# SwiGLU's first product by one level of Strassen's algorithm, its rows in five chunks, in a hybrid decoder trunk on one core

## The chip, the cores and the metric

One core of one Trainium2 chip runs the whole program. The metric is the device time of one execution in microseconds (us); the time before is the median of three runs. The engines are named as the profile names them: PE (TensorE matmul), PEld (TensorE weight load), DVE (VectorE), ACT (ScalarE), POOL (GpSimd), SP (SyncE, which issues the loads).

## The reference

A trunk of two layers over 512 tokens of width 1024, in float32. Layer one is a gated linear recurrence (RG-LRU) and a SwiGLU; then keys and values are computed once; layer two is a dilated attention and a second SwiGLU. The change is in both SwiGLUs:

```python
D_MODEL, SEQ = 1024, 512
FFN_HIDDEN = -(-8 * D_MODEL // (3 * 256)) * 256          # 2816

def swiglu(h, w_in, w_out):
    g, u = jnp.split(h @ w_in, 2, axis=-1)
    return (jax.nn.silu(g) * u) @ w_out

    ...
        h = h + swiglu(rms_norm(h, a_ffn_norm[i]), a_ffn_w_in[i], a_ffn_w_out[i])
```

## The kernel before

Everything is kept transposed: rows (features) on the 128 partitions, the 512 tokens along the free axis. The residual `h` is eight tiles 128x512, one for each 128 features. A float32 product is made of three products of a short float32 format: a value is split into a high half (a cast, ACT) and a low half (value minus high half, mostly DVE), and `mm3` issues high x high, high x low and low x high into one PSUM tile. `split` and `halve` make these halves for activations (`split` also multiplies by the norm's gain), `Stream._split` for weights.

The weights come as one long list of pieces (`add_pieces`), 128x1024 each or less. `Stream` loads them in that order through SP into two buffers `wr` (`_load`), two pieces ahead; one piece ahead it casts the high half `wh` on ACT (L92) and subtracts for the low half `wl` on DVE (L94), or on POOL for pieces marked `pool_lo`. There are three buffers each of `wh` and `wl`.

`swiglu` (L422) runs over 22 blocks `j` of 128 hidden rows. For each it computes the gate block and the up block, 8 x 3 = 24 matmuls 128x512 each (the first product), multiplies each by `rb` (the norm's factor for every token) on DVE, takes silu on ACT (L441), the product on POOL (L443), and splits the result into `gh[j]`, `gl[j]` (L203, L204). After all blocks `out_proj` (L238) runs over 8 blocks `m` of output features, each with 22 x 3 matmuls 128x512 (the second product), adds the PSUM tile to `h[m]` on DVE (L249) and calls `after(m)`, which splits and squares `h[m]` for the next stage or stores it. So an FFN has 1056 matmuls in the first product and 528 in the second, all of 512 columns, and the program has two FFNs.

The stage ahead of FFN1 is the `a_out` projection; its `after_a` splits `h[m]` into `xh`, `xl`. The stage ahead of FFN2 is `out_half(1)`, the second half of the attention's output projection (L823, added on DVE at L833), and then eight `split` calls. A tile framework orders each engine's instructions from the program text and priorities (weight splits run at high priority) and sets the semaphores; pools of buffers decide when a buffer is free again.

Of the kernel before, what the change touches and what calls it, by code (L numbers as in the profile page):

```python
# [23 lines left out]
T = 512  # L25
KB = 8
HID = 2816
HB = HID // 128
EPS = 1e-6
# [33 lines left out]

class Stream:
# [8 lines left out]
    def _load(self, i):  # L73
        ap = self.pieces[i][0]
# [3 lines left out]
        return [lambda c=c: self.nc.sync.dma_start(r[:, c], ap[:, c]) for c in self._cuts(i, w)]  # L78
# [4 lines left out]
    def _split(self, i):  # L83
        nc = self.nc
        r, w = self.raw.pop(i)
        hi = self.pool.tile([128, 1024], F32R, name=f"wh{i}", tag="wh")
        lo = self.pool.tile([128, 1024], F32R, name=f"wl{i}", tag="wl")
        self.parts[i] = (hi, lo)

        def do(c):  # L90
            with self.tc.high_priority():
                nc.scalar.copy(hi[:, c], r[:, c])  # L92
                eng = nc.gpsimd if self.pieces[i][1] else nc.vector
                eng.tensor_tensor(lo[:, c], r[:, c], hi[:, c].bitcast(F32), ALU.subtract)  # L94

        return [lambda c=c: do(c) for c in self._cuts(i, w)]

# [25 lines left out]
def trunk(tc, A, out):  # L123
# [3 lines left out]
    def mm3(ps, w, x, first, last):  # L127
        (wh, wl), (xh, xl) = w, x
        PE.matmul(ps, wh, xh, start=first, stop=False)  # L129
        PE.matmul(ps, wh, xl, start=False, stop=False)  # L130
        PE.matmul(ps, wl, xh, start=False, stop=last)  # L131
# [3 lines left out]
    def add_pieces(aps, pool_lo=False):  # L135
        start = len(pieces)
        pieces.extend((a, pool_lo) for a in aps)
# [4 lines left out]
    add_pieces([A["w_in"][m] for m in lru_order[2:]], True)  # L142
# [7 lines left out]
    p_f1 = ffn_pieces("f1_in", "f1_out")  # L150
    p_kv = add_pieces([A["w_kv"][i] for i in range(12)])
    p_q = add_pieces([A["w_q"][i] for i in range(24)], True)
    p_o = add_pieces([A["w_o"][i] for i in range(8)], True)
    p_f2 = ffn_pieces("f2_in", "f2_out")

    with tc.tile_pool(name="keep", bufs=1) as kp, tc.tile_pool(name="wts", bufs=3) as wp, \
# [96 lines left out]
        with tc.tile_pool(name="lru", bufs=2) as lp:  # L253
# [126 lines left out]
            hgh = [lp.tile([128, T], F32R, name=f"hgh{k}", bufs=1) for k in range(KB)]  # L380
            hgl = [lp.tile([128, T], F32R, name=f"hgl{k}", bufs=1) for k in range(KB)]
# [33 lines left out]
            def after_a(m):  # L415
                split(h[m], gain(C_AF, m), xh[m], xl[m])
                squares(m, lp, "q", 2)

            out_proj(p_aout, KB, KB, hgh, hgl, after_a)


        def swiglu(fp, p, after):  # L422
            gh = [fp.tile([128, T], F32R, name=f"gh{j}", bufs=1) for j in range(HB)]
            gl = [fp.tile([128, T], F32R, name=f"gl{j}", bufs=1) for j in range(HB)]
            for j in range(HB):
                pair = []
                for i in range(2):
                    ps = bank()
                    wh, wl = ws.get(p[0] + 2 * j + i)
                    for k in range(KB):  # L430
                        c = slice(128 * k, 128 * k + 128)
                        mm3(ps, (wh[:, c], wl[:, c]), (xh[k], xl[k]), k == 0, k == KB - 1)
                    pair.append(ps)
                    if j == 0 and i == 0:
                        r = norm_factors(fp)
                if j == 0:
                    rb = norm_rows(fp, r)
                g = fp.tile([128, T], F32, name="g")
                u = fp.tile([128, T], F32, name="u")
                V.tensor_tensor(g, pair[0], rb, ALU.mult)  # L440
                S.activation(g, g, AF.Silu)  # L441
                V.tensor_tensor(u, pair[1], rb, ALU.mult)  # L442
                G.tensor_tensor(u, u, g, ALU.mult)  # L443
                halve(u, gh[j], gl[j])
            out_proj(p[1], HB, 8, gh, gl, after)

        with tc.tile_pool(name="ffn1", bufs=2) as fp:
            fp = Pool(fp)

            def after_f1(m):  # L450
                split(h[m], gain(C_KV, m), xh[m], xl[m])
                squares(m, fp)

            swiglu(fp, p_f1, after_f1)


        with tc.tile_pool(name="att", bufs=2) as ap:
            ap = Pool(ap)
            attention(tc, A, ap, ws, dict(locals()))

        with tc.tile_pool(name="ffn2", bufs=2) as fp:
            fp = Pool(fp)

            def after_f2(m):
                nc.sync.dma_start(out[m], h[m])

            swiglu(fp, p_f2, after_f2)
# [9 lines left out]
def attention(tc, A, ap, ws, env):  # L477
# [388 lines left out]


    for _ in out_half(1, lambda m: env["squares"](m, ap, "qh", 3)):
        pass
    for m in range(8):  # L870
        split(h[m], gain(C_BF, m), xh[m], xl[m])
# [70 lines left out]
```

## Time and profile before

| what | value |
|---|---|
| time before, median of 3 runs (lowest, highest) | 1300.27 us (1297.78 to 1300.62) |
| the profiled execution | 1298.5 us |
| its span in the trace | 1296.7 us |
| PE busy | 1234.9 us, 95% |
| DVE busy | 733.3 us, 57% |
| ACT busy | 512.5 us, 40% |
| POOL busy | 234.3 us, 18% |
| moved by DMA | 112.98 MB, mean 87 GB/s |

The recurrent stage takes the first 150 us or so and `a_out` some 50 us behind it, FFN1 lies from about 200 to 560 us, keys, values and attention up to about 910, and FFN2 from there to the end. A row of a group reads: line, engine, operation, output and inputs, shape, count, then busy time, the mean of one in ns, and idle time ahead of it with what ended it. A matmul's own duration is longer than the distance to the next, since they are pipelined; what counts is the distance between starts, called pitch below.

### The profile page before, as it was taken

The page shows a single profiled execution, that of the slowest core. Times are in us where ns is not written, and L with a number is a line of the kernel's source. Part 1 is how long each engine was busy: PE and PEld are TensorE (multiplying, and loading weights), DVE is VectorE, ACT ScalarE, POOL GpSimd, SP SyncE. Part 2 cuts the span into 40 slices and gives each one's busy share as a digit, 9 for nine tenths or more (in the row PEclk, how much of TensorE's full clock was granted, in tenths as well). Part 3 has the DMA queues.
Part 4 walks back from the last instruction along what each step waited for, and adds up shares of the span by engine and source line. Part 5 has one row for each costly group of instructions (what it writes and reads, how often), then busy time and mean ns, then how long its engine had stood idle before and what let it go on. Part 6 is the DMA issues. An engine that isn't in the chain of part 4 may idle for free.

```text
span 1296.7 us, 14893 instructions
## 1 busy us (share of the span) xinstructions
PE 1234.9 (95%) x5634; PEld 1015.9 (78%) x5634; DVE 733.3 (57%) x1294; ACT 512.5 (40%) x950; POOL 234.3 (18%) x186
## 2 busy tenths in 40 slices
PE   6778899999999999999998899899999999999998
PEld 5556688888888888887877677789888888888887
DVE  7889865555544434367655666876755445552221
ACT  5466643233332223256444455654433322232120
POOL 1443100111111000010333354531111111110000
PEclk8888899999999999999998999799999999999999
DMA  5221222333333333332322211101223333233341
GB/s 179 83 65 49 66 98 92 92 94 96 98 98 98 90 99 97 104 108 97 114 82 65 82 50 65 33 17 34 86 93 98 98 98 96 90 93 108 106 122 53
DMA packets 35494, 112.98 MB, mean 87 GB/s; under 512 B 4320, under 2 KB 6496, under 8 KB 35424
## 3 DMA queue, kind: packets, MB, share of 16 engines
q1 hardware_dynamic: 34416, 110.17, 27.4%
q10 hardware_dynamic: 1008, 1.88, 0.5%
q8 instruction: 44, 0.72, 0.2%
q14 instruction: 26, 0.21, 0.1%
HBM read 108.89 MB, written 2.10 MB: 86 GB/s over the span
## 4 chain that ended last, share of the span: by engine, by line
PE 79%; DVE 14%; ACT 5%; issue 2%; DMA 0%; SPq 0%; POOL 0%; ACTq 0%; DVEq 0%; POOLq 0%
PE ps L131 22%; PE ps L130 22%; PE ps L129 22%; PE ps L633 3%; PE ps L634 3%; PE ps L635 3%; DVE kn L592 3%; DVE xc L328 1%; ACT junk L575 1%; DVE gated L377 1%; PE ps L708 1%; PE ps L778 1%; ACT wh L92 1%; DVE pr L763 1%; DVE cl L204 1%
## 5 line engine op out<-in xcount | busy, mean ns | idle before, releaser
L92 ACT CAST wh<-wr 128x1024 fp32r<-128x1024 f32 (+2 forms) x206 | 210.9, 1025 | 524.1 <-PE ps L130 452.7
L129 PE MATMUL ps<-xh,wh 128*128 128x512 f32 x896 | 356.6, 398 | 6.7 <-ACT xh L199 6.0
L131 PE MATMUL ps<-xh,wl 128*128 128x512 f32 x896 | 355.1, 396 | 0.0
L130 PE MATMUL ps<-xl,wh 128*128 128x512 f32 x896 | 352.5, 393 | 0.0
L94 DVE TENSOR_TENSOR wl<-wr,wh 128x1024 fp32r<-128x1024 f32 (+2 forms) x160 | 234.1, 1464 | 155.0 <-ACT wh L92 154.8
L129 PEld LDWEIGHTS ps<-xh,wh 128*128 128x128 f32 x896 | 170.5, 190 | 43.5 <-ACT xh L199 6.0
L130 PEld LDWEIGHTS ps<-xl,wh 128*128 128x128 f32 x896 | 170.4, 190 | 38.8 <-issue 0.7
L131 PEld LDWEIGHTS ps<-xh,wl 128*128 128x128 f32 x896 | 170.3, 190 | 37.5
L94 POOL TENSOR_TENSOR wl<-wr,wh 128x1024 fp32r<-128x1024 f32 x46 | 113.8, 2474 | 253.1 <-ACT wh L92 181.1
L443 POOL TENSOR_TENSOR u<-u,g 128x512 f32<-128x512 f32 x44 | 58.4, 1326 | 508.6 <-ACT wh L92 368.2
L129 PE MATMUL ps<-gh,wh 128*128 128x512 f32 x352 | 137.0, 389 | 0.0
L131 PE MATMUL ps<-gh,wl 128*128 128x512 f32 x352 | 136.9, 389 | 0.0
L130 PE MATMUL ps<-gl,wh 128*128 128x512 f32 x352 | 136.9, 389 | 0.0
L442 DVE TENSOR_TENSOR u<-ps,rb 128x512 f32<-128x512 f32 x44 | 30.4, 691 | 141.1 <-PE ps L131 141.1
L633 PE MATMUL ps<-wh,xh 128*128 128x512 f32 x224 | 93.6, 418 | 0.0
L635 PE MATMUL ps<-wh,xl 128*128 128x512 f32 x224 | 89.7, 401 | 0.0
L634 PE MATMUL ps<-wl,xh 128*128 128x512 f32 x224 | 89.7, 400 | 0.0
L130 PEld LDWEIGHTS ps<-gl,wh 128*128 128x128 f32 x352 | 66.1, 188 | 13.8
L131 PEld LDWEIGHTS ps<-gh,wl 128*128 128x128 f32 x352 | 66.1, 188 | 13.7
L129 PEld LDWEIGHTS ps<-gh,wh 128*128 128x128 f32 x352 | 66.1, 188 | 13.7
L440 DVE TENSOR_TENSOR g<-ps,rb 128x512 f32<-128x512 f32 x44 | 30.4, 691 | 66.5 <-PE ps L131 66.5
L203 ACT CAST gh<-u 128x512 fp32r<-128x512 f32 x44 | 27.3, 621 | 60.2 <-POOL u L443 60.2
(211 smaller groups left out, 1591.9 us busy)
## 6 DMA issues: line engine op xcount, KB each, us to landing
wr<-in_f_in SPq DMA_DIRECT2D x88, 512.0 KB, 3.5
wr<-in_f_out SPq DMA_DIRECT2D x32, 512.0 KB, 3.5
wr<-in_w_q SPq DMA_DIRECT2D x24, 512.0 KB, 3.5
wr<-in_w_in SPq DMA_DIRECT2D x14, 512.0 KB, 3.5
wr<-in_f_out SPq DMA_DIRECT2D x16, 384.0 KB, 3.1
wr<-in_w_kv SPq DMA_DIRECT2D x12, 512.0 KB, 3.5
wr<-in_a_out SPq DMA_DIRECT2D x8, 512.0 KB, 3.5
wr<-in_w_o SPq DMA_DIRECT2D x8, 512.0 KB, 3.5
```

Source lines behind the costliest of these rows:

```text
L92: nc.scalar.copy(hi[:, c], r[:, c])
L94: eng.tensor_tensor(lo[:, c], r[:, c], hi[:, c].bitcast(F32), ALU.subtract)
L129: PE.matmul(ps, wh, xh, start=first, stop=False)
L130: PE.matmul(ps, wh, xl, start=False, stop=False)
L131: PE.matmul(ps, wl, xh, start=False, stop=last)
L440: V.tensor_tensor(g, pair[0], rb, ALU.mult)
L442: V.tensor_tensor(u, pair[1], rb, ALU.mult)
L443: G.tensor_tensor(u, u, g, ALU.mult)
L592: V.scalar_tensor_tensor(dst[:, c], dst[:, c], r[:, nh * t + i:nh * t + i + 1], grow[:, g_row, :], ALU.mult, ALU.mult)
L633: PE.matmul(ps[t], xh[k][:, r], wh[:, c], start=k == 0, stop=False)
L634: PE.matmul(ps[t], xh[k][:, r], wl[:, c], start=False, stop=False)
L635: PE.matmul(ps[t], xl[k][:, r], wh[:, c], start=False, stop=k == 7)
```

## The change

The first product of a hidden block `j` becomes a "unit": the gate block and the up block are the two rows of a 2x2 block matrix, whose columns are the even and the odd input features k (blocks of 128); the tokens 0 to 255 and 256 to 511 are the two columns of the right side. Winograd's form of Strassen's algorithm makes the four results out of seven products: A11·B11, S1·T1, S2·T2, A12·B21, S3·T3, A22·T4, S4·B22, where S1 to S4 are sums of weight blocks and T1 to T4 sums of activation blocks. Each product is 4 pairs of k x 3 matmuls of 256 columns, so a unit has 84 matmuls 128x256 in place of 48 of 128x512.

The products are summed in two PSUM banks and a third takes A12·B21; three sums are copied out by ACT while their bank goes on accumulating (`copied`, 128x256: t1, t2, t3), and DVE adds them to the other products. The products A22·T4 and S4·B22 of a unit (`tail`) come after the first two products of the next unit (`head`). `rb` now multiplies the gate (up to its silu) and, for the up half, the output of the second product (`out_end`), so each output step takes two DVE steps, a product into `o` and an addition to `h[m]`, 40 times in an FFN, where before there were 8 additions.

For the weights of a unit DVE makes the four S sums (128x512 each) and their low halves (two of 128x1024), ACT their high halves. The low halves of A11, A12 and A22 are made without DVE: ACT writes the negated raw value's rounding (L135), and a DMA issued by POOL adds the raw weights to it, read once more from DRAM (L136: 512 KB into `wl`, 256 KB into `a2l`). For the activations `sums` makes T1 to T4 and their halves from pairs of `h` tiles; it takes the place of `split` ahead of both FFNs.

The hidden blocks come in chunks of 4, 5, 5, 4 and 4. The second product of chunk c runs between the units of chunk c+1, one or two output blocks `m` after each unit (matmuls 128x512, 12 or 15 to an output block); the last chunk's eight stand at the end. The pools of the stages overlap (`reuse_waits="tile"`, a pool on the right side for `hgh`, `hgl`, `gh`, `gl`).

```diff
+CHUNKS = (4, 5, 5, 4, 4)
...
+    def _load_unit(self, i):
+        g = self.pool.tile([128, 1024], F32, name=f"wr{i}", tag="wr", bufs=2)
+        u = self.unit_pool.tile([128, 1024], F32, name=f"ur{i}", tag="ur", bufs=1)
...
+    def _split_unit(self, i):
...
+        def negated_plus(lo, raw, ap):
+            nc.scalar.mul(lo, raw, -1.0)
+            nc.gpsimd.dma_start(lo, ap, accum_op=ALU.add)
...
+            (a11, a12), (a21, a22) = ([halves(t)[:, e] for e in range(2)] for t in (g, u))
+            negated_plus(a1l, g, self.pieces[i][0][0])
+            negated_plus(a2l, a22, halves(self.pieces[i][0][1])[:, 1])
+            nc.scalar.copy(a1h, g)
+            nc.scalar.copy(a2h, a22)
...
+            for n in range(2):
+                if n == 0:
+                    V.tensor_tensor(s[0][:, 0], a21, a22, ALU.add)
+                    V.tensor_tensor(s[0][:, 1], s[0][:, 0], a11, ALU.subtract)
+                else:
+                    V.tensor_tensor(s[1][:, 0], a11, a21, ALU.subtract)
+                    V.tensor_tensor(s[1][:, 1], a12, s[0][:, 1], ALU.subtract)
+                nc.scalar.copy(sh[n], s[n])
+                V.tensor_tensor(sl[n], s[n], sh[n].bitcast(F32), ALU.subtract)
...
     def ffn_pieces(wi, wo):
-        a = add_pieces([A[wi][b] for j in range(HB) for b in (j, HB + j)])
-        b = add_pieces([A[wo][m][:, c0:c1] for m in range(8) for c0, c1 in ((0, 1024), (1024, 2048), (2048, 2816))])
-        return a, b
...
+                steps.append(("unit", j, add_pieces([(A[wi][j], A[wi][HB + j])], "unit")))
+                while c and done * size < 8 * (n + 1):
+                    steps.append(out_step(c - 1, done))
+                    done += 1
...
+        def sums(pool, m, c):
...
+            for i in range(2):
+                S.activation(x[i], h[m - 1 + i], AF.Copy, scale=gain(c, m - 1 + i))
...
+            V.tensor_tensor(t1, x[0][:, b], x[0][:, a], ALU.subtract)
+            V.tensor_tensor(tt[:, 0], x[1][:, b], t1, ALU.subtract)
+            V.tensor_tensor(tt[:, 1], x[1][:, b], x[0][:, b], ALU.subtract)
+            V.tensor_tensor(tt[:, 2], x[1][:, a], tt[:, 0], ALU.subtract)
+            halve(x[0][:, a], h1[:, a], l1[:, a])
+            halve(t1, h1[:, b], l1[:, b])
+            halve(tt, th, tl)
+            halve(x[1], h2, l2)
...
+            def head(w):
+
+                pa, pc = bank("PT"), bank("mm")
+                product(pa, w["A11"], "B11", True, False)
+                t1 = copied(pa, "t1")
+                product(pc, w["S1"], "T1", True, False)
+                return pa, pc, t1
+
+            def middle(w, pa, pc, t1):
+
+                pb = bank("S")
+                product(pa, w["S2"], "T2", False, False)
+                t2 = copied(pa, "t2")
+                product(pb, w["A12"], "B21", True, True)
+                g = fp.tile([128, T], F32, name="gt")
+                u = fp.tile([128, T], F32, name="ut")
+                V.tensor_tensor(g[:, a], pb[:, a], t1, ALU.add)
+                product(pa, w["S3"], "T3", False, False)
+                t3 = copied(pa, "t3")
+                V.tensor_tensor(u[:, b], pc[:, a], t3, ALU.add)
+                return w, pa, pc, t2, g, u
+
+            def tail(w, pa, pc, t2, g, u):
+                product(pa, w["A22"], "T4", False, True)
+                product(pc, w["S4"], "B22", False, True)
+                V.tensor_tensor(g[:, b], pc[:, a], t2, ALU.add)
+                V.tensor_tensor(g, g, rbs[0], ALU.mult)
+                S.activation(g, g, AF.Silu)
+                V.tensor_tensor(u[:, a], pa[:, a], g[:, a], ALU.mult)
+                V.tensor_tensor(u[:, b], u[:, b], g[:, b], ALU.mult)
...
+            def out_end(ps, m, last):
+
+                o = fp.tile([128, T], F32, name="o", tag="o", bufs=1)
+                V.tensor_tensor(o, ps, rbs[0], ALU.mult)
+                V.tensor_add(h[m], h[m], o)
+                if last:
+                    after(m)
...
+                if last and m < 2:
+                    out_part(ps, parts, c, range(n - 1))
+                    held.append((ps, parts, c, [n - 1]))
+                    if m == 1:
+                        for i, x in enumerate(held):
+                            out_part(*x)
+                            out_end(x[0], i, last)
```

Three places show how the instructions move. First, ACT's own order in the middle of FFN1. Before, for two pieces of weights and one block (`wh` the high half of a piece, `g` the silu, `gh` the high half of the gated block):

```order
L92 CAST wh_1683<-wr_1642 128x1024
L441 ACTIVATE g<-g 128x512
L92 CAST wh_1714<-wr_1681 128x1024
L203 CAST gh_1399<-u 128x512
L92 CAST wh_1753<-wr_1712 128x1024
L441 ACTIVATE g<-g 128x512
```

Now, a whole unit of a later chunk: `a2l` and `wl` are the negated values that an accumulating DMA completes, `sh` the high halves of the sums, `gt` the silu of the unit before, `t_2616` the copy of t2, `wh_2718` a piece of the second product.

```order
L146 CAST a2h<-ur_2649 128x512
L135 ACTIVATE a2l<-ur_2649 128x512
L157 CAST sh<-s 128x1024
L565 ACTIVATE gt<-gt 128x512
L157 CAST sh<-s 128x1024
L535 COPY t_2616<-ps 128x256
L135 ACTIVATE wl_2675<-wr_2648 128x1024
L145 CAST wh_2674<-wr_2648 128x1024
L283 CAST gh<-ut 128x512
L535 COPY t_2645<-ps 128x256
L114 CAST wh_2718<-wr_2672 128x512
```

Four instructions a block became eleven a unit, and the copy of t2 comes behind the silu of the unit before and the second `sh` cast; the negated copy into `wl_2675`, ahead of the accumulating DMA, comes behind that copy.

Second, PE's order between A12·B21 (`xh`, `xl` of odd k against `wh`, `wl`) and S3·T3 (`th`, `tl` against `sh`, `sl`) of a unit in FFN1; before, PE had 24 matmuls 128x512 in a row here for each block, such as these.

```order
L130 MATMUL ps<-xl_82,wh_2694 128x512
L131 MATMUL ps<-xh_74,wl_2695 128x512
L129 MATMUL ps<-xh_75,wh_2694 128x512
L130 MATMUL ps<-xl_83,wh_2694 128x512
L131 MATMUL ps<-xh_75,wl_2695 128x512
```

And now:

```order
L196 MATMUL ps<-xl_87,wh_3354 128x256
L197 MATMUL ps<-xh_79,wl_3355 128x256
L195 MATMUL ps<-gh,wh_3399 128x512
L196 MATMUL ps<-gl,wh_3399 128x512
L195 MATMUL ps<-th,sh 128x256
L196 MATMUL ps<-tl,sh 128x256
```

Two matmuls of the chunk before's second product (`gh`, `gl`) stand between the two products; S3·T3, which accumulates in the bank that t2 is copied from, follows them.

Third, DVE's order at the end of `out_half(1)`, ahead of FFN2. Before, from the last of the eight additions to `h` on (`xl` the low halves of the activations, `ssum` the sum of squares, `nrv` and `nry` steps of the norm):

```order
L833 TENSOR_TENSOR h_71<-h_71,ps 128x512
L200 SCALAR_TENSOR_TENSOR xl_86<-h_70,par,xh_78 128x512
L94 TENSOR_TENSOR wl_7627<-wr_7573,wh_7626 128x1024
L212 TENSOR_TENSOR ssum<-ssum,sq 128x512
L200 SCALAR_TENSOR_TENSOR xl_87<-h_71,par,xh_79 128x512
L222 TENSOR_SCALAR nrv<-ps 128x4
L190 TENSOR_SCALAR nry<-nrv 128x4
```

Now, from the same addition on (`t_9260` is T1 and `tt` are T2 to T4 of the third pair, `tl` their low halves, `x` the rows of `h` times the gain):

```order
L1020 TENSOR_TENSOR h_71<-h_71,ps 128x512
L284 TENSOR_TENSOR xl_83<-x,xh_75 128x512
L509 TENSOR_TENSOR t_9260<-x 128x256
L511 TENSOR_TENSOR tt<-x 128x256
L510 TENSOR_TENSOR tt<-x,t_9260 128x256
L512 TENSOR_TENSOR tt<-x,tt 128x256
L292 TENSOR_TENSOR ssum<-ssum,sq 128x512
L284 TENSOR_TENSOR xl_84<-x,xh_76 128x256
L284 TENSOR_TENSOR xl_84<-t_9260,xh_76 128x256
L284 TENSOR_TENSOR tl<-tt,th 128x768
```

Behind the last addition the sums of the third and (after these rows) the fourth pair are still to come, with sums of weights of the second unit among them, where before two low halves and one piece of weights were left.

More of the change, by code (lines that the diff above doesn't have):

```diff
@@ L73, in _load @@
     def _load(self, i):
-        ap = self.pieces[i][0]
+        ap, kind = self.pieces[i]
+        if kind == "unit":
+            return self._load_unit(i)
         r = self.pool.tile([128, 1024], F32, name=f"wr{i}", tag="wr", bufs=2)
@@ L84, in _split @@
         nc = self.nc
+        if self.pieces[i][1] == "unit":
+            return [lambda: self._split_unit(i)]
         r, w = self.raw.pop(i)
@@ new lines, in trunk, with after_f2 @@
+        swiglu(fp, gp, f1, after_f1)
+        close_g()
+        close_f()
+        with tc.tile_pool(name="att", bufs=2, reuse_waits="tile") as ap:
+            ap = Pool(ap)
+            finish = attention(tc, A, ap, ws, dict(locals()))
+        close_f, fp = swiglu_pools()
+        finish(lambda m: squares(m, fp, "o"))
+        for m in range(KB):
+            sums(fp, m, C_BF)
+        close_g, gp = right_pool(tc, "gates")
+        def after_f2(m):
+            nc.sync.dma_start(out[m], h[m])
@@ L470 @@
+        swiglu(fp, gp, f2, after_f2)
+        close_g()
+        close_f()
 N_KN = 4
@@ L865, in attention, with finish @@
     drain(o0)
[L868 to L871, printed above, removed]
+    def finish(after):
+        for _ in out_half(1, after):
+            pass
+    return finish
 def _layout(a):
```

172 lines of the change are left out of this document (117 added, 55 removed).

## Prediction

> **What bounds the kernel now.** I read the totals by engine, the chain of waits, busy time by stretch (columns: stretch; length; PE, PEld, DVE, ACT, POOL busy with counts; granted clock; DMA share; GB/s), and then the groups by shape.
>
> ```profile
> span 1296.7 us, 14893 instructions
> PE 1234.9 (95%) x5634; PEld 1015.9 (78%) x5634; DVE 733.3 (57%) x1294; ACT 512.5 (40%) x950; POOL 234.3 (18%) x186
> PE 79%; DVE 14%; ACT 5%; issue 2%; DMA 0%; SPq 0%; POOL 0%; ACTq 0%; DVEq 0%; POOLq 0%
> 320.00:440.00 120.00, 120.00 (x526) 98.47 (x525) 61.13 (x55) 35.69 (x44) 14.32 (x11) 1.00 0.31 93
> 440.00:560.00 120.00, 120.00 (x530) 99.29 (x530) 41.41 (x46) 32.91 (x39) 1.93 (x1) 1.00 0.32 96
> 912.00:935.00 23.00, 23.00 (x102) 18.88 (x101) 19.51 (x25) 13.11 (x19) 2.41 (x1) 1.00 0.33 98
> 1060.00:1180.00 120.00, 120.00 (x526) 98.47 (x526) 58.21 (x55) 35.09 (x43) 14.87 (x11) 1.00 0.31 96
> SPq L78 <- DVE wl L94: 709.6, 147, 17.3
> ```
>
> TensorE is never idle in either FFN at full granted clock, not at the start of the second one either (912 to 935). DVE is half busy, ACT less than a third. The load queue waits for buffers (last row, 709.6 us), not the other way. So the FFNs cost matmuls times pitch: 120/526 = 0.2281 us for the first product, 120/530 = 0.2264 for the second.
>
> **The core of the change.** Per block of the hidden rows, 48 matmuls of 512 columns become 84 of 256 columns (7 products x 4 pairs x 3). Removed: 2 x 22 x 48 = 2112 x 0.2281 = 481.7 us. Added: 3696. Their pitch stands in the attention stage (columns: start, duration, what):
>
> ```profile
> 783.61 0.28 PE L129 MATMUL ps<-ph,vh 128*128 128x256 f32 x1
> ...
> 784.20 0.28 PE L131 MATMUL ps<-ph,vl 128*128 128x256 f32 x1
> 784.32 0.22 PE L129 MATMUL ps<-ph,vh 128*128 128x128 f32 x1
> 738.10 0.19 PEld L130 LDWEIGHTS ps<-kl,qh 128*128 128x128 f32 x1
> 738.21 0.19 PEld L131 LDWEIGHTS ps<-kh,ql 128*128 128x128 f32 x1
> ```
>
> Six start between 783.61 and 784.32: 0.118 us each, 3696 x 0.118 = 436.1. Core: 436.1 - 481.7 = **-45.6 us**. The core breaks even at a pitch of 481.7/3696 = 0.130; at 0.1141 (half of the wide pitch) it would give -60. I take the measured 0.118. The second product keeps its 1056 matmuls.
>
> **The other engines in a steady unit** (chunks 1 to 4: one unit and on average 24 matmuls of the second product). Prices:
>
> ```profile
> 561.52 1.23 DVE L94 TENSOR_TENSOR wl<-wr,wh 128x1024 fp32r<-128x1024 f32 x1 [0.17 <-ACT wh L92]
> L94 DVE TENSOR_TENSOR wl<-wr,wh 128x768 fp32r<-128x768 f32 x16 | 15.3, 958 | 0.0
> L440 DVE TENSOR_TENSOR g<-ps,rb 128x512 f32<-128x512 f32 x44 | 30.4, 691 | 66.5 <-PE ps L131 66.5
> L753 DVE CUSTOM_DVE_ANT_0 pr<-ps,near 128x256 f32<-128x256 f32 x24 | 9.9, 416 | 4.1 <-PE ps L131 4.0
> L92 ACT CAST wh<-wr 128x1024 fp32r<-128x1024 f32 x186 | 195.1, 1050 | 471.8 <-PE ps L130 406.7 <-PE ps L635 25.7 <-issue 14.3
> L441 ACT ACTIVATE g<-g 128x512 f32<-128x512 f32 x44 | 27.6, 628 | 0.0
> 603.55 0.37 ACT L571 COPY kn<-ps 128x256 f32<-128x256 f32 x1 [0.39 <-PE ps L635]
> L833 DVE TENSOR_TENSOR h<-h,ps 128x512 f32<-128x512 f32 x16 | 10.9, 683 | 4.1 <-PE ps L131 4.1
> L212 DVE TENSOR_TENSOR ssum<-ssum,sq 128x512 f32<-128x512 f32 x28 | 21.0, 749 | 2.3 <-ACT sq L211 2.2
> 555.00:580.00 25.00, 25.00 (x118) 20.56 (x117) 15.10 (x44) 13.69 (x21) 6.08 (x9) 1.00 0.42 134
> wr<-in_f_in SPq DMA_DIRECT2D x88, 512.0 KB, 3.5
> h<-in_x SPq DMA_DIRECT2D x8, 256.0 KB, 5.3
> ```
>
> - PE: 84 x 0.118 + 24 x 0.2264 = 15.3 us.
> - DVE: four S sums of 0.69, two low halves of 1.23, five 256-column steps of 0.42, the multiply by `rb` and the low half of the gated rows at 0.69 each: 8.7; plus, for 1.8 pieces of the second product, low halves of about 0.7 and the two steps of `out_end` (2 x 0.69): 12.4 us. Hidden behind 15.3, with 2.9 to spare. These rows replace the two low halves, three other DVE steps and a GpSimd product per block of before.
> - ACT: 4 x 1.05 (a1 twice, `sh` twice), 4 x 0.63 (a22 twice, silu, gh), 3 x 0.37, 1.8 casts: 8.9 us. Hidden in sum.
> - Traffic: 1 MB of raw blocks, 0.75 MB read again by the accumulating DMAs of L136, 0.5 MB of the second product: 2.3 MB in 15.3 us, about 148 GB/s; 134 GB/s went beside a gapless PE (row 555 to 580, share 0.42). Nothing for bandwidth.
> - SP only issues later: its queue already waits for buffers. GpSimd loses its product and issues two accumulates per unit.
>
> So sums hide; chains may not. These are the terms that count.
>
> **Loop through ACT.** The partial sum t2 has to be copied out of PSUM by ACT before S3·T3 may go on in that bank. In the ACT order shown above (ffn1) the copy `t_2616` stands behind the previous unit's silu and behind the second `sh` cast; silu waits for the previous unit's S4·B22, which PE finishes just ahead of S2·T2. From the end of S4·B22: hand-over about 0.2 (the cast at 561.52 started 0.17 after its releaser), add of 256 columns 0.42, times `rb` 0.69, silu 0.63, cast 1.05, copy 0.37: 3.36 us. PE has S2·T2 and A12·B21 (24 x 0.118 = 2.83) and the two matmuls of 512 columns that the PE order puts there (0.45): 3.28 us, less where none stand there. Missing with a second hand-over: 0.1 to 0.5 a unit, taken 0.3 x 40 = **+12**. Ends: 0 (a cast that runs early) and 0.8 x 42 = +34.
>
> **Starts.** FFN1: each pair of rows of `h` needs casts, five sums or products and four low halves, before its T's exist. Behind the last matmul of `a_out` DVE has some 10.6 us (add, sum of squares, one pair of about 4.0, lower halves of the pair before it); PE has 64 narrow matmuls that don't need the last pair (7.6): **+3** to 3.5. FFN2: DVE has 8 adds (5.5), 7 sums of squares (5.2), four pairs of 4.0 (16.1), and the S sums and low halves of unit 0 in the same queue (5.2): 32 us, from 3 us after the start of `out_half(1)`. PE has 96 x 0.228 = 21.9 and some 50 narrow ones (5.9). 35 - 27.8 = 7, and ACT works as long in turns with DVE: **+10**, ends 0 and 16 (nothing narrow goes ahead, and the norm behind it). Before had no gap there (912 to 935).
>
> **Tails.** The last unit's chain (add 0.42, `rb` 0.69, silu 0.63, two products 0.84, cast 0.63, low half 0.69, and hand-overs of 0.1 to 0.2) is about 4.6 us beside 18 held matmuls of 4.1; the last `out_end` adds a DVE step of 0.69: **+2.7** for both FFNs. FFN1 to K/V: the split of `h[7]` comes behind one more DVE step per row block: **+1**.
>
> **The accumulates.** No row of before has a DMA of GpSimd's queue. In a cycle with two second-product pieces the negated copy into `wl_2675` stands behind the t2 copy, ends at about 10.2 us of the cycle, and the next unit's third matmul wants the sum at 15.9 (pieces of 12 matmuls) or 17.2 (of 15): 5.7 or 7.0 us for issue, read, add and landing. The plain load of 512 KB takes 3.5, the slowest load row 5.3 (at the start, under load). Lower end 0. Upper end: the slowest row and an ACT-to-queue step as large as the plain load's 3.5 gives 8.8, which is rival C. Nearest row is the plain one, and I take **+4** for some late ones.
>
> Sum: -45.6 + 12 + 3.3 + 10 + 2.7 + 1 + 4 = -12.6 against the profiled execution's 1298.5 (its span and 1.8 around it): 1285.9. The median of the runs stands 1.8 above the profiled one: 1287.7, say **1288**.
>
> **Rivals.**
> B, the cover holds: no t2 wait and no late accumulate; 16 us less, **1272**; with the starts covered too, 1298.5 - 45.6 + 1.8 = 1255. For it: 2.9 us of slack on DVE, 6 on ACT. Against: both chains above are within 0.5 us of their cover.
> C, the accumulating DMA comes late, and the change is **slower**. The third matmul of a unit waits, with all of PE's queue behind it. 14 cycles of each FFN have the short allowance, half 5.7 and half 7.0. At 7.5 us from ACT's end to PE: 2 x (7 x 1.8 + 7 x 0.5) = +32, instead of the 4: **1316**; at 8.5 +60: 1344. It decides from about 6.9 us, where 14 x 1.2 eats the gain. For it: an unseen kind of transfer that reads and adds in its target. Against: 3.5 us for the same bytes.
> The Trainium skill, "SBUF — State Buffer", says in its trap "DVE blocks DMA" that GpSimd writes the descriptors of such a DMA and stands still while DVE holds their shared port; that would be C's cause. The same section of the Trainium skill names copies for it, not the two-source sums that DVE does here; no run here shows it yet.
> D, a narrow matmul costs more than its half, since each has a weight load of its own: it decides from a pitch of 0.130, and with loads one after another the products take 3696 x 0.19 = 702 for 482: **1520**. The two loads 0.11 apart, each 0.19 long, and six matmuls at 0.118 speak against it.
> The Trainium skill, "TensorE: Matmul & The Clock Gate", Back-to-back issue gap, would have it so: it gives a sustained spacing of about 81 ns at 128 columns and 131 at 512. On a line between them (98 ns at 256, an estimate) 3696 x 0.098 against 2112 x 0.131 makes the change 85 us slower. The trace disagrees (118 and 228 ns), and the measurement decides.
> E, DVE becomes the bound. In the recurrent stage, beside GpSimd's work, its 512-column steps were longer than 0.69:
>
> ```profile
> L376 DVE TENSOR_TENSOR gated<-gated,tau 128x512 f32<-128x512 f32 x8 | 8.3, 1082 | 1.5 <-ACT tau L370 1.5
> L443 POOL TENSOR_TENSOR u<-u,g 128x512 f32<-128x512 f32 x44 | 58.4, 1326 | 508.6 <-ACT wh L92 368.2 <-ACT g L441 105.2 <-DVE u L442 35.2
> ```
>
> At 1.3 times its price a unit is 16.1, 0.8 over PE in 36 units: +29 for the 12: **1305**; it decides from 15.3/12.4 = 1.23. Against: GpSimd's products (L443) are gone from the FFNs.
>
> **Chances.** Forecast 0.42 (its own range 1272 to 1301), B 0.26, C 0.17, E 0.08, D 0.02, others 0.05. One measurement tells 0.2% (2.6 us) from no change. Faster: 0.36 of the forecast's, B, 0.03 of the rest: 0.65. Same: 0.04 of the forecast's, 0.02 of C, 0.02 of E: 0.08. Slower 0.27. The range goes from B's middle between clean and covered to C at 7.5 us: 1260 to 1317, leaving out about 0.08 on each side.
>
> **What would show it.** Right: narrow matmuls 0.118 apart; PE busy in the FFNs about 46 us less; ACT's t2 copy as what ended idle time ahead of S3·T3, a few tenths each; a gap of about 10 us ahead of FFN2's first unit, released by DVE's `tl`. Wrong: waits of the third matmul of units for a DMA (C), DVE above 95% in the steady stretch (E), a narrow pitch over 0.13 (D), no idle time but the starts (B).

## The result: slower by 1.5%

The changed kernel takes 1319.41 us (median of 4 runs, 1317.22 to 1319.57), against 1300.44 before (1297.78 to 1301.14): a ratio of 1.0146, 95% interval 1.0128 to 1.0164. The forecast was 1288, with a range from 1260 to 1317.

From the page of the changed kernel, span, busy times and the two large DMA queues (packets, MB, share of 16 engines' span):

```profile
span 1317.4 us, 19514 instructions
PE 1218.1 (92%) x7218; PEld 1066.1 (81%) x7218; DVE 954.6 (72%) x1870; ACT 701.7 (53%) x1322; POOL 269.1 (20%) x233
q1 hardware_dynamic: 39024, 110.17, 27.3%
q0 software_dynamic: 29568, 34.61, 17.9%
wr<-in_f_in SPq DMA_DIRECT2D x44, 512.0 KB, 4.1
wl<-in_f_in POOLq DMA_DIRECT2D x44, 512.0 KB, 6.7
```

Busy time by stretch (columns as before): the start of FFN1, its steady part, the passage to keys and values. First the kernel before, then the changed one:

```profile
197.00:239.00 42.00, 42.00 (x187) 34.28 (x186) 22.39 (x37) 15.46 (x19) 3.90 (x3) 1.00 0.28 88
256.00:556.00 300.00, 300.00 (x1317) 246.97 (x1316) 133.02 (x129) 86.14 (x105) 23.08 (x18) 1.00 0.32 97
556.00:606.00 50.00, 50.00 (x231) 40.99 (x230) 36.93 (x120) 30.12 (x76) 6.08 (x9) 1.00 0.33 105
```

```profile
197.00:239.00 42.00, 32.94 (x243) 31.17 (x242) 28.91 (x60) 25.59 (x38) 6.17 (x6) 0.92 0.68 156
256.00:556.00 300.00, 293.03 (x1967) 267.32 (x1966) 207.68 (x337) 148.83 (x231) 33.83 (x33) 0.99 0.61 137
556.00:606.00 50.00, 44.44 (x189) 35.36 (x188) 43.30 (x99) 31.42 (x67) 7.15 (x9) 0.93 0.38 112
```

And the largest waits of TensorE that are new (us in total, times, longest):

```profile
PE ps L197 <- DMA wl<-in_f_in: 14.7, 13, 2.6
PE ps L195 <- ACT t L535: 9.7, 8, 5.0
PE ps L820 <- DVE rtmp L696: 4.6, 1, 4.6
```

TensorE, gapless before, is idle for 9.1 of FFN1's first 42 us, for 7.0 of the 300 after them, and for 5.6 of the 50 at the passage to keys and values, and its granted clock dips in the first and the third (0.92, 0.93). 34.61 MB of accumulating DMAs (q0) take 17.9% of the DMA engines' span, 110.17 MB of plain loads 27.3%: twice the time for a byte.

To say where the time went I added up, over a stretch of the trace, the distances between starts of neighbouring matmuls, each less its pitch (0.1183 us for 256 columns, 0.2281 for 512, 0.1 for others; a row of the timeline that stands for several matmuls counts as that many). This excess holds idle time, slow clock and all. "Start" is the first 42 us from an FFN's first matmul, "rest" what follows up to its last; for the kernel before, whose first product is longer, the start is 60 us. The last column is the time from FFN1's last matmul to the attention's last.

| kernel | start 1 | rest 1 | start 2 | rest 2 | K/V, attention |
|---|---|---|---|---|---|
| before | 0.5 | -0.1 | 0.7 | -0.1 | 343.4 |
| changed | 13.4 | 15.0 | 13.7 | 15.8 | 351.7 |

Starts +25.9, rests +31.0, keys and values +8.3, together 65; the core gives 44.5 back (3696 x 0.1183 - 2112 x 0.2281 = -44.5). That leaves 20.7, and the spans differ by 20.7.

### The profile page after: what moved, and what is told of

It is laid out like the page before. It is cut to its first block, busy times and chain, and to the rows that moved or that the text cites. A ratio compares the mean times of both kernels' runs of the same rounds, so it can differ in the third digit from the quotient of the medians.

```text
span 1317.4 us, 19514 instructions
## 1 busy us (share of the span) xinstructions
PE 1218.1 (92%) x7218; PEld 1066.1 (81%) x7218; DVE 954.6 (72%) x1870; ACT 701.7 (53%) x1322; POOL 269.1 (20%) x233
## 3 DMA queue, kind: packets, MB, share of 16 engines
q1 hardware_dynamic: 39024, 110.17, 27.3%
q0 software_dynamic: 29568, 34.61, 17.9%
## 4 chain that ended last, share of the span: by engine, by line
issue 44%; PE 25%; DVE 16%; POOL 6%; ACT 5%; DMA 3%; POOLq 0%; SPq 0%; ACTq 0%; DVEq 0%
PE ps L196 5%; PE ps L197 5%; PE ps L195 5%; POOL a2l L136 4%; DVE kn L779 3%; PE ps L820 3%; PE ps L821 3%; PE ps L822 3%; POOL wl L136 2%; DMA wl<-in_f_in 1%; DVE xc L409 1%; ACT junk L762 1%; DVE gated L458 1%; DVE wl L116 1%; ACT wh L114 1%
## 5 line engine op out<-in xcount | busy, mean ns | idle before, releaser
L197 PE MATMUL ps<-xh,wl 128*128 128x256 f32 (+1 forms) x544 | 179.8, 330 | 14.7 <-DMA wl<-in_f_in 14.7
L195 PE MATMUL ps<-xh,wh 128*128 128x256 f32 (+1 forms) x544 | 180.2, 332 | 8.1 <-ACT xh L279 5.9
L196 PE MATMUL ps<-xl,wh 128*128 128x256 f32 (+1 forms) x544 | 178.2, 328 | 1.5 <-DVE xl L284 1.3
L136 POOL DMA_DIRECT2D a2l<-in_f_in x44 | 53.0, 1205 | 434.7 <-ACT a2l L135 386.9
L196 PEld LDWEIGHTS ps<-xl,wh 128*128 128x128 f32 x544 | 105.7, 194 | 12.4 <-DVE xl L284 2.1
L158 DVE TENSOR_TENSOR sl<-s,sh 128x1024 fp32r<-128x1024 f32 x88 | 106.9, 1217 | 1.8 <-ACT sh L157 1.7
L195 PE MATMUL ps<-th,sh 128*128 128x256 f32 x352 | 103.0, 293 | 3.3 <-ACT t L535 3.1
L195 PE MATMUL ps<-xh,sh 128*128 128x256 f32 x352 | 99.6, 283 | 1.1 <-ACT sh L157 1.1
L197 PE MATMUL ps<-th,sl 128*128 128x256 f32 x352 | 99.9, 284 | 0.0
L196 PE MATMUL ps<-tl,sh 128*128 128x256 f32 x352 | 99.7, 283 | 0.0
L196 PE MATMUL ps<-xl,sh 128*128 128x256 f32 x352 | 99.0, 281 | 0.0
L197 PE MATMUL ps<-xh,sl 128*128 128x256 f32 x352 | 98.8, 281 | 0.0
L116 DVE TENSOR_TENSOR wl<-wr,wh 128x512 fp32r<-128x512 f32 (+2 forms) x104 | 86.0, 830 | 14.7 <-ACT wh L114 14.5
```

Of the source, the lines that this page charges most:

```text
L136: nc.gpsimd.dma_start(lo, ap, accum_op=ALU.add)
L158: V.tensor_tensor(sl[n], s[n], sh[n].bitcast(F32), ALU.subtract)
L195: PE.matmul(ps, wh, xh, start=first, stop=False, **k)
L196: PE.matmul(ps, wh, xl, start=False, stop=False, **k)
L197: PE.matmul(ps, wl, xh, start=False, stop=last, **k)
```

## The experiments

All ratios are to runs of the kernel before on the same chip, with their 95% intervals.

**The pitch.** `narrow`, the kernel before with two matmuls of 256 columns for one of 512 (its output is not the reference's; number and shape of the matmuls are as said):

```diff
...
-                        mm3(ps, (wh[:, c], wl[:, c]), (xh[k], xl[k]), k == 0, k == KB - 1)
+                        for t in (slice(0, 256), slice(256, 512)):
+                            mm3(ps[:, t], (wh[:, c], wl[:, c]), (xh[k][:, t], xl[k][:, t]), k == 0, k == KB - 1)
```

> Edit, to the kernel before: each of the 2112 matmuls of 512 columns of the first products is made as two of 256 columns (4224), nothing else. Theory (the pitch is as read, 0.118): 4224 x 0.118 = 498 against 482, 17 us more, about 1317. Rival (each narrow matmul pays a weight load that the pitch of the attention stage hid): at 0.130 it is 67 us more, 1367, and the core of the change is worth nothing.

Measured: 1313.32, ratio 1.0103 (1.0087 to 1.0119), 14.0 us more than 1299.35. (481.7 + 14.0)/4224 = 0.1174 us for each narrow matmul. In its steady stretch TensorE has no idle time, though the weight loads fill the whole of it:

```profile
320.00:440.00 120.00, 120.00 (x1021) 120.00 (x1020) 57.30 (x53) 34.34 (x43) 14.09 (x11) 1.00 0.29 93
```

Rival D is out; the core is worth its 45 us.

**The accumulating DMAs.** Five edits in `_split_unit`:

```diff
 no_acc:
-            nc.gpsimd.dma_start(lo, ap, accum_op=ALU.add)
 acc_plain:
-            nc.gpsimd.dma_start(lo, ap, accum_op=ALU.add)
+            nc.gpsimd.dma_start(lo, ap)
 lo_dve (lo_pool: nc.gpsimd in place of nc.vector):
-            negated_plus(a1l, g, self.pieces[i][0][0])
-            negated_plus(a2l, a22, halves(self.pieces[i][0][1])[:, 1])
...
+            nc.vector.tensor_tensor(a1l, g, a1h.bitcast(F32), ALU.subtract)
+            nc.vector.tensor_tensor(a2l, a22, a2h.bitcast(F32), ALU.subtract)
 a2_dve: the second pair of lines alone
```

> Edit: the accumulating DMAs of the units are left out (the low halves of A11, A12 and A22 hold the negated rounding alone, so the output is not the reference's); everything else stays. Theory (DMA): their waits (14.7 us in 13 waits of a unit's third matmul), the slower clock behind these waits, and the loads that they hold up (wr landed 8.5 us after its issue in the first chunk, with the DMA engines full) make most of the 65 us that the FFNs lose against the pitch of their matmuls: 25 to 35 us less, 1285 to 1295. Rival (order on ACT and DVE, starts): only the named waits go, about 15 us, 1304. Second rival: nothing, as other waits take their place, 1315 or more.

> Edit: the low halves of A1 and A22 by a DVE subtraction (128x1024 and 128x512) in place of ACT's negated copy and the accumulating DMA. DVE gets 1.9 us more a unit: 14.3 of 15.3 us in a steady unit, 10.6 against PE's 9.9 in the first chunk; ACT loses 1.7 us and the traffic 33 MB. Theory (DMA): 15 to 30 us less, 1290 to 1304, a little behind the kernel without accumulates. Rival (DVE becomes the bound): 1319 or more, DVE over 93% busy in the steady stretch and the waits of PE are for DVE.

> Edit: the same subtractions on POOL (2.5 us for 128x1024, about 1.4 for 128x512, 3.9 of 15.3 us a unit). Theory (DMA): as without accumulates, 20 to 30 us less, 1290 to 1300, since POOL has nothing else there. Rival (POOL's sums slow DVE: the low half of 1024 columns took 1.54 us on the mean before, 1.23 alone): DVE goes from 12.4 to 14 or 15 us a unit, and no more than 10 us come back, 1310.

> Edit: only the low half of A22 (128x512) by a DVE subtraction; the low half of A1 stays with the accumulating DMA. No matmul was seen to wait for a2l, so what it costs can only be traffic (256 KB in pieces of 512 bytes) and its place ahead of wl on POOL's queue. Theory (the accumulates of A1 come late because those of A22 share queue and DMA engines with them): most of the gain of all low halves on DVE, 1308 to 1311. Rival (only A1's own time counts): within 4 us of 1319.

> Edit, to the changed kernel: POOL's DMAs of the low halves copy and don't add (the low halves of A11, A12 and A22 are the raw values, so the output is not the reference's); bytes, queue and order stay. Theory (the adding makes them late: 17.9% of the DMA engines' time for 34.6 MB against 27.3% for 110.2 MB by plain loads, and 6.7 us from issue to landing against 4.1): landing about 4.5 us and 15 to 27 us less, 1292 to 1304. Rival (bytes, POOL's issue and the place behind ACT's queue make them late): within 5 us of 1319.

| kernel | us | ratio (95%) | start 1 | rest 1 | start 2 | rest 2 | K/V, attention |
|---|---|---|---|---|---|---|---|
| no_acc | 1292.58 | 0.9943 (0.9928 to 0.9958) | 6.4 | 4.4 | 12.9 | 4.9 | 352.2 |
| acc_plain | 1295.71 | 0.9981 (0.9966 to 0.9996) | 9.8 | 4.7 | 13.2 | 5.5 | 351.9 |
| lo_dve | 1307.26 | 1.0048 (1.0029 to 1.0067) | 11.9 | 4.5 | 17.7 | 10.2 | 351.8 |
| a2_dve | 1319.84 | 1.0160 (1.0136 to 1.0183) | 12.9 | 11.8 | 18.3 | 11.8 | 351.8 |
| lo_pool | 1341.67 | 1.0322 (1.0307 to 1.0337) | 15.8 | 19.4 | 21.3 | 22.6 | 351.8 |

Without accumulates the rests fall by 21.5 us of the 31.0, start 1 by 7. With the same bytes in the same queue, not added, the rests fall by 20.6: it is the adding. What start 1 owes to the accumulates is less sure, since `sq_own` below, which keeps them, has 6.4 us less there too. Of the 9.3 us that the rests keep in `no_acc`, 7.0 are no waits: the wide matmuls of the second product start 0.2326 us apart, 0.2268 in the kernel before (means over FFN1), and the narrow ones 0.119. Why the wide ones are slower is not known. The DMA queue and the issues of `acc_plain`, in the view whose rows of the changed kernel stand above:

```profile
q0 software_dynamic: 29568, 34.61, 10.8%
wr<-in_f_in SPq DMA_DIRECT2D x44, 512.0 KB, 3.7
wl<-in_f_in POOLq DMA_DIRECT2D x44, 512.0 KB, 3.9
```

6.7 us to landing become 3.9, 17.9% become 10.8%, and the raw loads land 0.4 us sooner. For a plain DMA of this queue the Trainium skill ("DMA: Bandwidth & Descriptors", Anatomy of one DMA) fits 2.0 us and a time that grows with the bytes, 3.2 us for 512 KB, an estimate from its formula. The plain ones agree about with it (3.9); those that add took 2.8 more.

The named waits for `wl` sum to only 14.7 us; part of the rest comes behind them. The timeline of the changed kernel on TensorE (start, duration, what, and idle time ahead with what ended it) around the longest of them:

```profile
311.60 0.28 PE L196 MATMUL ps<-xl,wh 128*128 128x256 f32 x1
314.48 0.58 PE L197 MATMUL ps<-xh,wl 128*128 128x256 f32 x1 [2.60 <-DMA wl<-in_f_in]
314.86 0.42 PE L195 MATMUL ps<-xh,wh 128*128 128x256 f32 x1
315.08 0.41 PE L196 MATMUL ps<-xl,wh 128*128 128x256 f32 x1
...
317.00 0.41 PE L196 MATMUL ps<-xl,sh 128*128 128x256 f32 x1
317.21 0.34 PE L197 MATMUL ps<-xh,sl 128*128 128x256 f32 x1
317.39 0.28 PE L195 MATMUL ps<-xh,sh 128*128 128x256 f32 x1
```

After a wait of 2.6 us the next twelve matmuls start 0.21 to 0.22 apart, at half the pace, until 317.2: 1.2 us more. In the changed kernel's FFNs 94 distances between narrow matmuls are of 0.19 to 0.24 us, in `narrow` two; some 9 us in all.

All low halves on DVE leave no wait for a DMA and clear most of the rests too (the 10.2 hold a wait of 3.1 for DVE's `ut` at 979, still in the first chunk), but cost 4.0 in start 2, where the waits are for DVE and ACT; only 12 of the 27 us come back. On POOL they slow DVE. The S sum of L152 in the changed kernel, and then in `lo_pool`:

```profile
L152 DVE TENSOR_TENSOR s<-ur 128x512 f32<-128x512 f32 x44 | 30.4, 690 | 37.2 <-DMA ur<-in_f_in 37.2
L152 DVE TENSOR_TENSOR s<-ur 128x512 f32<-128x512 f32 x44 | 78.5, 1783 | 39.3 <-DMA ur<-in_f_in 39.3
```

`a2_dve` is no faster: 7 us less in the rests, 4 more in the starts. So its rival had the time, but A22's accumulates are not free: they cost those 7 us in the rests, and what DVE does in their place costs 4 in the starts.

**Keys and values, and the factor `rb`.** Two edits, and a third that joins one with `lo_dve`:

```diff
 sq_own, after_f1:
-            squares(m, fp, "o")
+            squares(m, fp, "ut", 2)
 rb_gate, tail and out_end (rb_dve: this and lo_dve):
                 S.activation(g, g, AF.Silu)
+                V.tensor_tensor(g, g, rbs[0], ALU.mult)
...
-                V.tensor_tensor(o, ps, rbs[0], ALU.mult)
-                V.tensor_add(h[m], h[m], o)
+                V.tensor_add(h[m], h[m], ps)
```

> Edit: at the end of the first FFN the squares of h go into the idle buffers of the tag ut (two) and no longer into the one buffer o that out_end also writes. Theory (one buffer paces the last chunk): in the changed kernel an output block of the last chunk takes 3.6 us on DVE and ACT in turns (o at 569.65, 573.25, 576.84), though PE makes one in 12 x 0.228 = 2.7, so the norm of the next stage starts some 8 us late and PE falls 8.6 us behind between 576 and 597. With a buffer of its own the period falls to about 2.8 us and 5 to 8 us come back: about 1312 us. Rival (sum of DVE's and ACT's work in that stretch, whatever the buffer): within 2 us of 1319.

> Edit: the norm's factor is applied a second time to the gate behind silu (22 steps of 0.69 us an FFN) and no longer to each output of the second product (40 steps of 0.69); out_end is one addition. The last chunk's period on DVE falls from 3.5 to 2.8 us. Theory (DVE's work at the end of FFN1 delays the next stage by 8 us, and DVE's work in the steady units makes loads late): 8 to 14 us less, 1305 to 1311. Rival (the chain ahead of the second product gets longer by 0.7 us in every unit): 1319 or more.

> Edit: both low halves on DVE and the norm's factor on the gate behind silu. DVE has 12.4 + 1.9 - 0.5 = 13.8 us of a steady unit of 15.3. If the gains are of different places (12 us for the low halves, 8 to 14 for the factor) they add: 1293 to 1300. Rival (both are the same slack of DVE): no more than 4 us under the better one alone.

| kernel | us | ratio (95%) | start 1 | rest 1 | start 2 | rest 2 | K/V, attention |
|---|---|---|---|---|---|---|---|
| sq_own | 1313.45 | 1.0110 (1.0082 to 1.0137) | 7.0 | 16.3 | 14.0 | 16.7 | 349.9 |
| rb_gate | 1304.83 | 1.0037 (1.0023 to 1.0052) | 9.2 | 13.4 | 15.0 | 11.5 | 346.9 |
| rb_dve | 1303.86 | 1.0033 (1.0024 to 1.0043) | 14.4 | 5.4 | 21.1 | 8.8 | 342.3 |

`sq_own` came out at the time that its theory gave, and the theory is still wrong: in the stretch that it speaks of 1.8 us came back, and 6.4 came in FFN1's start, which the edit doesn't touch. That start differs by some 7 us from program to program, and here perhaps from run to run: the four runs went from 1310.28 to 1319.28. DVE's own rows of the changed kernel show what an output block of the last chunk costs there:

```profile
569.65 0.69 DVE L581 TENSOR_TENSOR o<-ps,rb 128x512 f32<-128x512 f32 x1
570.38 0.69 DVE L582 TENSOR_TENSOR h<-h,o 128x512 f32<-128x512 f32 x1
571.86 0.75 DVE L280 SCALAR_TENSOR_TENSOR xl<-h,par,xh 128x512 fp32r<-128x512 f32 x1 [0.79 <-ACT xh L279]
572.53 0.68 DVE L292 TENSOR_TENSOR ssum<-ssum,sq 128x512 f32<-128x512 f32 x1
573.25 0.69 DVE L581 TENSOR_TENSOR o<-ps,rb 128x512 f32<-128x512 f32 x1
```

3.6 us a block, where TensorE makes one in 12 x 0.2281 = 2.7. Four steps of 0.7 fill 2.8 of it, already more than 2.7; in these rows the other 0.8 is a wait for ACT's `xh`, and in the block ahead of them DVE has two low halves of pieces of weights, 1.2 us each. So DVE cannot keep up with any number of buffers. One step less (`rb_gate`), which also frees the buffer, brings 4.8 us here, the buffer alone 1.8: it is mostly the work. `chunk2` below agrees: with the same steps, but five hidden blocks in its last chunk and so 15 x 0.2281 = 3.4 us of TensorE for each output block, it has 6.6 us less here.

The 4.8 are only a third of what `rb_gate` brings: start 1 falls by 4.2 and the rests by 5.9. The gains of `rb_gate` and `lo_dve` don't add: `rb_dve` is 1 us under `rb_gate`, as its rival said, and most of what it gains in the rests and behind them it loses in the starts (14.4 and 21.1).

**The starts.** Three edits:

```diff
 sums_out (the T sums and their halves):
-            V.tensor_tensor(t1, x[0][:, b], x[0][:, a], ALU.subtract)
-            V.tensor_tensor(tt[:, 0], x[1][:, b], t1, ALU.subtract)
-            V.tensor_tensor(tt[:, 1], x[1][:, b], x[0][:, b], ALU.subtract)
-            V.tensor_tensor(tt[:, 2], x[1][:, a], tt[:, 0], ALU.subtract)
...
+            halve(x[0], h1, l1)
 chunk2:
-CHUNKS = (4, 5, 5, 4, 4)
+CHUNKS = (2, 5, 5, 5, 5)
 start_free: sums_out, no_acc, and
-        finish(lambda m: squares(m, fp, "o"))
+        finish(lambda m: m or squares(m, fp, "o"))
... (the same in after_a, ahead of FFN1)
```

> Edit, to the changed kernel: the sums T1 to T4 of the activations are left out ahead of both FFNs (T1 is the right half of the even rows, T2 to T4 the right half of the odd rows, so the output is not the reference's); the halves of h are made as before, matmuls and all else stay. DVE loses four steps of 256 columns and a low half of 768 for each pair: 4 x 2.6 = 10.6 us at each start, ACT 4 x 0.8. Theory (DVE's and ACT's work at the starts, ahead of and among the first chunk's units, makes most of the 14 and 19 us that PE loses there, stalls and slow clock together): 15 to 22 us less, 1297 to 1304. Rival (loads and accumulates set the starts): within 5 us of 1319.

> Edit, to the changed kernel: chunks of 2, 5, 5, 5, 5 blocks in place of 4, 5, 5, 4, 4, so that matmuls of the second product stand among the units from the third unit on, not from the fifth. Theory (units without second-product matmuls beside them are starved: PE needs 9.9 us, while loads, accumulates and the queues of ACT and DVE need more): about half of what is lost at the starts comes back, 8 to 14 us, 1305 to 1311. Rival (the loss is that of the first unit and of the T sums alone, and the last chunk's longer pieces cost nothing): within 4 us of 1319.

> Edit, to the changed kernel: left out are the T sums (as before, T1 to T4 are halves of the rows themselves), seven of the eight squares of h ahead of each FFN and all accumulating DMAs, so the output is not the reference's; matmuls, S sums, copies and chunks stay. Theory (work of DVE and ACT and the accumulates, each enough to hold the start alone): the excess over the matmuls' pitch in the first 42 us falls from 14.5 and 15.3 to under 5 in both FFNs; together with the 21 us of the rest without accumulates about 1275 us. Rival (a unit without second-product matmuls beside it shows its own chain: copies out of PSUM, sums, silu, the norm's diagonal): 8 us or more stay at each start, 1283 to 1290.

| kernel | us | ratio (95%) | start 1 | rest 1 | start 2 | rest 2 | K/V, attention |
|---|---|---|---|---|---|---|---|
| sums_out | 1315.64 | 1.0122 (1.0109 to 1.0135) | 11.9 | 13.4 | 14.0 | 12.2 | 351.6 |
| chunk2 | 1325.84 | 1.0193 (1.0177 to 1.0210) | 9.3 | 19.3 | 16.8 | 20.6 | 345.1 |
| start_free | 1279.51 | 0.9850 (0.9837 to 0.9864) | 2.9 | 3.4 | 7.1 | 3.5 | 350.2 |

The expectations' 14.5 and 15.3 take each row of the timeline for one matmul; counted as here they are 13.4 and 13.7. Without the T sums alone the starts stayed: other steps came first (in start 1 a wait of 3.9 us for a high half of `h` on ACT, in start 2 one of 4.6 for a low half on DVE). Fewer units ahead of the second product made it slower (both rests rose); that theory fell. Without T sums, squares and accumulates together the starts lose 17.1 of the 25.9 us that the change added there. In the first 45 us or so of FFN1 TensorE of `start_free` is nearly gapless at full clock, with DVE at 30 of 45 us:

```profile
195.00:240.00 45.00, 44.27 (x345) 42.08 (x344) 30.45 (x63) 28.55 (x45) 0.00 (x0) 1.00 0.27 83
```

So units with no second-product matmuls beside them run well in start 1 when these three are gone: they are what holds start 1, not the bare chain of a unit. In start 2, 7.1 us stay, between theory and rival; 3.4 of them are three waits for the halves of the last rows of `h`, behind the eight additions. How the work's share divides among T sums, squares and accumulates is not settled, since each alone hides behind the others.

The longest single wait of the changed kernel's FFNs, in start 1, is none of the forecast's. Behind an S1·T1 of the first chunk TensorE waits with A22·T4 for a copy on ACT (L535). The timeline, with the rows of ACT and of the load:

```profile
216.85 0.33 SPq L124 DMA_DIRECT2D wr<-in_f_in  x1
219.72 0.38 ACT L535 COPY t<-ps 128x256 f32<-128x256 f32 x1
225.33 1.06 ACT L135 ACTIVATE wl<-wr 128x1024 fp32r<-128x1024 f32 x1 [5.23 <-DMA wr<-in_f_in]
226.29 1.03 ACT L145 CAST wh<-wr 128x1024 fp32r<-128x1024 f32 x1
227.22 0.36 ACT L535 COPY t<-ps 128x256 f32<-128x256 f32 x1
227.64 0.58 PE L195 MATMUL ps<-th,a2h 128*128 128x256 f32 x1 [5.00 <-ACT t L535]
```

The negated copy for a unit to come stands ahead of the copy out of PSUM and waits 5.2 us for its load, issued at 216.85 and landed 8.5 us later, with two accumulates beside it.

**A version that beats both.** Accumulates only in the first chunk's units, where DVE is short; DVE's low halves in all others; the factor on the gate:

```diff
-            negated_plus(a1l, g, self.pieces[i][0][0])
-            negated_plus(a2l, a22, halves(self.pieces[i][0][1])[:, 1])
+            if self.pieces[i][1] == "unit_a":
+                negated_plus(a1l, g, self.pieces[i][0][0])
+                negated_plus(a2l, a22, halves(self.pieces[i][0][1])[:, 1])
...
+            if self.pieces[i][1] == "unit":
+                nc.vector.tensor_tensor(a1l, g, a1h.bitcast(F32), ALU.subtract)
+                nc.vector.tensor_tensor(a2l, a22, a2h.bitcast(F32), ALU.subtract)
...
-                steps.append(("unit", j, add_pieces([(A[wi][j], A[wi][HB + j])], "unit")))
+                steps.append(("unit", j, add_pieces([(A[wi][j], A[wi][HB + j])], "unit_a" if c == 0 else "unit")))
 hybrid_c2: and CHUNKS = (2, 5, 5, 5, 5)
 hybrid_t: and
-                S.copy(t, ps[:, a])
+                with tc.high_priority():
+                    S.copy(t, ps[:, a])
```

> Edit: the norm's factor on the gate; low halves by accumulating DMA in the first chunk's four units (where DVE has the sums of the start to do) and by DVE in all later ones. With all low halves on DVE the steady stretch of FFN1 had no idle PE at all, with the accumulates PE was idle for 5.5 us there, and the other way about at the start of FFN2 (idle 14.6 against 8.6 us between 903 and 1000). Theory (each place keeps the better of the two): 1304 less 9 for steady stretches and 2 to 5 for the clock behind them: 1290 to 1297, faster than the kernel before. Rival (the loads of the first chunk run into the units of the second): 1300 to 1304.

> Edit: the same with chunks of 2, 5, 5, 5, 5. If starved units cost as in the run with these chunks alone, it gives what that gives, 4 to 10 us under the one with chunks of 4: 1283 to 1292. Rival (units three and four then have DVE low halves while DVE still works off the start): same as with chunks of 4, within 3 us.

> Edit, to the hybrid (norm's factor on the gate, accumulates in the first chunk only): the copies t1 to t3 get the high priority that the splits of weights have, so that ACT's order puts them ahead of work on a unit to come. Theory (head-of-line blocking on ACT: the copy of t waited 5.0 us behind a cast that waited for its load): 3 to 6 us less than the hybrid's 1293.6, about 1289. Rival (the copies wait for PE and hold up the splits instead): 1294 or more.

| kernel | us | ratio (95%) | start 1 | rest 1 | start 2 | rest 2 | K/V, attention |
|---|---|---|---|---|---|---|---|
| hybrid | 1293.64 | 0.9952 (0.9940 to 0.9964) | 9.9 | 5.2 | 14.5 | 6.1 | 344.5 |
| hybrid_c2 | 1296.89 | 0.9979 (0.9969 to 0.9989) | 12.4 | 4.9 | 18.1 | 7.5 | 345.4 |
| hybrid_t | 1292.72 | 0.9946 (0.9934 to 0.9959) | 10.7 | 5.3 | 15.4 | 6.3 | 345.9 |

The hybrid is 0.5% faster than the kernel before and 2% faster than the change as made; its steady stretch is gapless at full clock and its passage to keys and values nearly so:

```profile
256.00:556.00 300.00, 300.00 (x2001) 272.86 (x2000) 236.78 (x368) 133.54 (x208) 0.00 (x0) 1.00 0.33 98
556.00:606.00 50.00, 48.76 (x221) 38.54 (x219) 41.93 (x128) 34.88 (x94) 6.09 (x9) 1.00 0.33 102
```

The copies' place in ACT's order is worth nothing that can be measured (0.9946 against 0.9952): in start 1 a wait of 4.3 us for DVE's `ut` took the place of those for copies. Shorter first chunks lose here as they did alone.

## Why the prediction was wrong

- The core: -45.6 forecast, -44.5 by the pitches, and `narrow` confirms it. D is out, and E is out in the steady stretch (DVE 207.68 of 300 us). The second product was taken to cost what it did; its wide matmuls at 0.2326 for 0.2268 us make some 6 us (1056 x 0.0058), a term that the sum lacks.
- **The accumulates, forecast +4: measured 24 (`acc_plain`) to 27 us (`no_acc`), 21 of them in the rests.** This is the step that failed most. I priced a transfer that adds by a plain load of the same bytes (3.5 us) as the nearest row. A plain DMA of that queue does take 3.9; the adding makes it 6.7, slows the loads beside it, and the waits behind it bring the slow clock, which I had no term for. Rival C had the place (third matmul of a unit) and the point where it decides (6.9 us) about right, and 1316 for 7.5. That this lies so near 1319.41 is luck in part: it charges the accumulates 32 us, and the other terms that were too small make up for the loop through ACT that was too large. Its cause by the Trainium skill, "SBUF — State Buffer", the trap "DVE blocks DMA", is not what the runs show: with DVE as busy as in the changed kernel (955.5 us in `acc_plain`, 954.6 in the changed one), the plain DMAs of the same queue land in 3.9 us.
- **The starts, forecast +13: measured +25.9** (up to 7 of them shared with the accumulates). I counted DVE's work up to the last pair, and took the units behind it as covered. DVE and ACT are still behind when the first chunk's units run (`start_free`); that wide matmuls beside these units would cover it is not shown, and `chunk2` was slower. In the starts, too, the clock is lower (0.92).
- **Tails and keys and values, forecast +3.7: measured 8.3** for the latter alone. I looked at the order behind the last block, not at the rate of the last eight, 3.6 us on DVE for 2.7 on TensorE.
- **The loop through ACT, forecast +12: mis-sized, too large.** TensorE's waits for the copies are 9.7 us in 8 waits, one of them the 5.0 at 222, which has another cause. Of the steady units only four waited, 1.9 us together (0.4 in FFN1's rest and 1.5 in FFN2's). The copy is nearly always within the two wide matmuls' cover that I had counted at the edge.

So three terms too small, one too large and one missing: 33 us forecast against 65, and the sign turned.

## What to carry to other kernels

Fewer matmul columns are worth their pitch only where the work that feeds them has slack at the ends too: look at the starts and the last chunk by rate, block for block, not at the sum over the steady stretch. A DMA that adds is not a load of the same size: price it by a run, and where an engine has slack, let it subtract. Where two ways to make the same operand load different resources, choose by stage: with the factor on the gate that brought `rb_dve`'s 1303.86 us down to 1293.64, and +1.5% became -0.5%.

## What the runs showed of the hardware

- An accumulating DMA of 512 KB landed 6.7 us after its issue, the same without adding 3.9. All 88 of the queue (512 and 256 KB, 34.61 MB) took 17.9 against 10.8% of the DMA engines' span.
- After a wait of 2.6 us narrow matmuls ran 0.21 us apart for 2.7 us, then again 0.118. The Trainium skill, "TensorE: Matmul & The Clock Gate", What's actually happening, has a gate that halves the clock after an idle window of about 3.4 us and gives it back after as much activity. The halving agrees with the trace; here a shorter wait was enough.
- A narrow matmul with a weight load of its own costs 0.117 us, and a load unit that is busy all the time (120.00 of 120) held up nothing.
